# Expert sums in x's place, a fourth buffer for weight parts, and modulation chunks loaded two ahead from ScalarE's queue

## The chip, the cores and the metric

The kernel runs on one core of a Trainium2 chip. A core has TensorE (PE, matmul), VectorE (DVE), ScalarE (ACT), GpSimd (POOL) and SyncE (SP); SP computes nothing here and only issues DMA transfers. Sixteen DMA engines move data between DRAM and the on-chip memory SBUF. The metric is the device time of one execution, in microseconds; less is better.

## The reference

A two-layer network in float32 on T = 256 tokens of width D = 2048, for one sequence. From a conditioning vector c come modulation vectors (shift, scale, gate), as silu(c) times large matrices.

```
def first_block(x, c, ...):
    mod = silu(c) @ w_ada + b_ada
    sh1, sc1, ga1, sh2, sc2, ga2 = split(mod, 6)
    x = x + ga1 * hybrid_mixer(rmsnorm(x) * (1 + sc1) + sh1)
    x = x + ga2 * peer(rmsnorm(x) * (1 + sc2) + sh2)
    return rmsnorm(x, g_final)

def peer(h):   # 8 heads, 128 x 128 product keys, 16 experts kept for each head
    act = gelu(h @ peer_u[chosen].T) * routing_weight
    return act @ peer_v[chosen]
```

Behind it stand an S5 state-space layer with a gated output, then an attention layer with compressed, selected and window branches; each has modulation vectors of its own (mod_w0, mod_w1, kv_mod_w). peer_u and peer_v hold 16,384 experts of 2,048 numbers each, 128 MB apiece.

## The kernel before

The experts are not gathered: the kernel computes all 16,384 of them and multiplies what was not chosen by zero. The work runs in this order (us of the profiled execution): first modulation (0 to 110), the mixer (110 to 590), queries and top-k (590 to 720), gate products of the first expert groups beside the routing tables (720 to 1030), the **V stage** (1030 to 2376), the addition of the expert sums to x (`home`, to 2440), S5 (to 2690), its gate and output and the keys and values (to 3040), attention (to 3616).

In the V stage 16 expert groups alternate: `u_group` (x times peer_u, gelu, routing weight) of a group ahead, then `v_group` (activations times peer_v). `mix` builds a group's activations from gates and a routing table `wd` that comes back from DRAM: GpSimd multiplies (L909), ScalarE rounds (L911), GpSimd takes the rest (L913). The sums of the experts lie in `acc` (tile `vacc`, 16 KB for each partition), to which DVE adds what PE left in PSUM (L937); `home` transposes them and adds them to x.

A float32 weight is used as two rounded parts. `half` (L335) loads 128x1024 numbers, 512 KB, into a `raw` buffer (L339, issued by SP); ScalarE casts it to `wh` (L342); DVE takes the rest, `wl` = raw - wh (L346). PE multiplies by both: in `step_b` by wh on 512 columns (L357) and by wl on 256 (L358), eight such pairs for a half; in `v_group` with three products of 512 columns (L928 to L930), four such triples for a half. I call a 128x1024 piece of a weight a half. `raw` has four buffers, wh and wl three each, `graw` two.

Modulation is computed in the background. `gemv` (L284) is a generator that loads a 128x1024 **chunk** of a modulation matrix into a `graw` buffer (L299, issued by SP) and then adds it, scaled, to the row sums `gacc` on DVE (L312), or multiplies it on PE (L293) in the stage that has no gacc pool. `tick`, called once for every two halves, advances it by a rate: 1.5, later 3 steps in the mixer, and in the V stage as many as spread what is left over 205 ticks. Beside it, `s5_tables` builds 16 tables for S5 in one tile `tb` on DVE and stores each to DRAM (L1193).

The program is written in this order, and a tile scheduler then orders each engine's instructions by priority and estimated time; each engine works through its own list in order, and an instruction that waits holds all that stand behind it.

Of the kernel before, what the change touches and what calls it, by code (L numbers as in the profile page):

```python
# [9 lines left out]
F = mybir.dt.float32  # L10
# [67 lines left out]
COLS = {}  # L78
PAUSE = 2


# [75 lines left out]
class K:  # L157
    def __init__(self, tc, A, dbg=None):
        self.tc, self.nc, self.A = tc, tc.nc, A
        self.dbg = dbg or {}  # L160
        self.full = True
        self.nw, self.pool_share, self.srate = 0, 0, 1
        self.bg, self.side, self.par, self.loads = [], [], [], []
        self.loaded, self.gate, self.gp, self.hold, self.mid = None, None, None, None, False
        self.rate, self.owed, self.sowed, self.towed, self.slow = 1.5, 0.0, 0.0, 0.0, None

# [115 lines left out]


    def gemv(self, w, blocks, which, bias, out, big=False):  # L284
        nc = self.nc
        for b in blocks:
# [9 lines left out]
            for k in range(KD):  # L296
                if not big:
                    raw = self.sb.tile([128, 1024], F, name="graw", tag="graw", bufs=2)
                    nc.sync.dma_start(raw, w[128 * k:128 * k + 128, c0])  # L299
                else:  # L300
                    if k % 4 == 0:
                        rt = self.xs(F).rearrange("p a b t -> p (a b t)").rearrange("p (a c) -> p a c", a=4)
                        self.loads.append(
                            nc.sync.dma_start(rt, w[128 * k:128 * k + 512, c0].rearrange("(a p) c -> p a c", a=4)))
                    raw = rt[:, k % 4]
                ck = self.cact[:, 16 * which + k:16 * which + k + 1]
                if acc is None:
                    columns(ck.to_broadcast([128, 32]), raw, k == 0, k == KD - 1)
                elif k == 0:
                    nc.vector.tensor_scalar(acc, raw, ck, None, op0=OP.mult)  # L310
                else:
                    nc.vector.scalar_tensor_tensor(acc, raw, ck, acc, op0=OP.mult, op1=OP.add)  # L312
                if k < KD - 1:
                    yield True
# [20 lines left out]
    def half(self, src, i):  # L335
        nc = self.nc
        s = self.sb.tile([128, 1024], F, name="raw", tag="raw", bufs=4)
        with self.after(self.gate):
            self.loaded = nc.sync.dma_start(s, src[:, 1024 * i:1024 * i + 1024])  # L339
        h = self.sb.tile([128, 1024], R, name="wh", tag="wh", bufs=3)  # L340
        l = self.sb.tile([128, 1024], R, name="wl", tag="wl", bufs=3)
        nc.scalar.copy(h, s)  # L342
# [405 lines left out]
    def _peer(self, x):  # L748
# [6 lines left out]
        xk = [x[:, k] for k in range(KD)]  # L755
        self.normed(xk, self.rstd(self.accx, D), g, mod[:, 48:64], hs)
        kt = self.t8()
        ktf = kt.rearrange("p a b -> p (a b)")
# [100 lines left out]
        def router():  # L859
# [3 lines left out]
            for q in range(64 + LAG):  # L863
# [11 lines left out]
                if q >= LAG:  # L875
# [10 lines left out]
                    if r % 4 == 3:  # L886
                        nc.sync.dma_start(wd[r // 4], tb.rearrange("p i t -> p (i t)"))
                yield True
# [27 lines left out]
        def v_group(gv, ap):  # L916

            for dq in range(4):
# [13 lines left out]
                for t in range(2):  # L932
                    s = acc[:, t, 512 * dq:512 * dq + 512]
                    if gv == 0:
                        nc.scalar.copy(s, pp[t])
                    else:
                        nc.vector.tensor_add(s, s, pp[t])  # L937
                if gv == 15:
                    self.par.append(home(dq))

        def home(dq):

            yield True
            for k in range(4 * dq, 4 * dq + 4):
                p = self.pm()[:, :T]
                for t in range(2):
                    nc.tensor.transpose(p[:, 128 * t:128 * t + 128], acc[:, t, 128 * k:128 * k + 128], self.ident)
                nc.vector.scalar_tensor_tensor(x[:, k], p, mod[:, 80 + k:81 + k], x[:, k], op0=OP.mult, op1=OP.add)
                self.accx = self.ssq(None if k == 0 else self.accx, x[:, k], k == KD - 1)
# [24 lines left out]
        self.ph = ctx.__enter__()  # L974
        acc = self.ph.tile([128, 2, D], F, name="vacc")
        self.slow = self.s5_tables()
        self.use_pool(self.ph if GP[2] else None)
        if self.full:
            self.pace("m1", VR)
        self.pool_share = VP  # L980
        for gv in range(16):
            nx = None
            if gv + 1 < 16:
                aps[gv + 1] = self.xs()
                nx = mix(gv + 1, gq[gv + 1], aps[gv + 1])
                self.side.insert(0, nx)
# [46 lines left out]
    def s5_setup(self):  # L1033
# [59 lines left out]
        def cmul(o, xr, xi, y):  # L1093

            wr, wi, yr, yi = wide(xr), wide(xi), y[:, :, 0], y[:, :, 1]
            t = self.sb.tile([128, 1024], F, name="graw", tag="graw", bufs=2)
            t = t.rearrange("p (k j c) -> p k j c", k=16, j=4)
# [72 lines left out]
    def s5_tables(self):  # L1170
        nc = self.nc
        for jj in range(16):
# [19 lines left out]
            nc.scalar.activation(tb, tb, AF.Sin, scale=-6.283185)  # L1192
            nc.sync.dma_start(self.s5d[jj][:, :1024], tb.rearrange("p i a b -> p (i a b)"))  # L1193
            yield True
# [193 lines left out]
    def _nsa(self, x):  # L1388
# [27 lines left out]
        def compress(i):  # L1416
            p = self.pm()
            for h in range(4):
                w = sb.tile([128, 1024], F, name="raw", tag="raw", bufs=4)
                nc.sync.dma_start(w, A["cmp_w1"][i][:, 1024 * h:1024 * h + 1024])  # L1420
# [193 lines left out]
```

## Time and profile before

| | |
|---|---|
| median of 3 runs | 3625.65 us (3624.92 to 3626.92) |
| the profiled execution | 3617.7 us, its span 3616.0 us |
| PE busy | 3294.4 us, 91% of the span |
| DVE busy | 2652.5 us, 73% |
| ACT busy | 1700.7 us, 47% |
| POOL busy | 1066.7 us, 29% |
| granted PE clock, mean | 0.961 |
| DMA | 832.47 MB, 230 GB/s over the span |

Busy time counts executing instructions; issuing a DMA is not among them. A matmul's end is modelled, so PE may be slower than it could be while it counts as busy. Idle time of an engine matters only where the engine that sets the pace then waits for it.

### The profile page before, as it was taken

Reading aid. Unit: us, or ns where it says so; the run is one execution under the profiler, and the core shown is the slowest. Engines: PE = TensorE matmul, PEld = TensorE weight load, DVE = VectorE, ACT = ScalarE, POOL = GpSimd, SP = SyncE. Lnnn points to the kernel's source line nnn. Section 1 sums busy time; section 2 is a strip of 40 time slices with the busy share of each in tenths; the row PEclk is TensorE's granted clock in tenths of the full one; section 3 lists DMA queues with packets and bytes.
Section 4 is the critical chain, followed back from the end, with each engine's and each line's share of the span. In section 5 each row is a group of like instructions: output and inputs, shape, how many; then the busy total and the mean of one; then the engine's idle time right before and its main releaser. Section 6 shows DMA issues by size and latency. Waiting matters only on the chain.

```text
span 3616.0 us, 50453 instructions
## 1 busy us (share of the span) xinstructions
PE 3294.4 (91%) x18446; PEld 2726.2 (75%) x18446; DVE 2652.5 (73%) x4072; ACT 1700.7 (47%) x2789; POOL 1066.7 (29%) x892
## 2 busy tenths in 40 slices
PE   4988778999999999999999989988989989999998
PEld 1676666878777777777777777767878878888886
DVE  4778987997657778887777767779886565666665
ACT  1534544455544444554444433354545544555553
POOL 1123345666522121211211233035452320122223
PEclk7999989999999999999999999989999999999999
DMA  9697676567779888888888878744435556444444
GB/s 398 235 301 252 203 234 228 163 223 262 243 250 314 300 281 291 293 285 279 293 286 278 293 268 269 267 158 139 147 127 186 186 167 198 160 155 149 159 143 144
DMA packets 260409, 832.47 MB, mean 230 GB/s; under 512 B 25792, under 2 KB 66880, under 8 KB 257472
## 3 DMA queue, kind: packets, MB, share of 16 engines
q1 hardware_dynamic: 258096, 829.11, 68.0%
q8 instruction: 145, 2.38, 0.3%
q14 instruction: 104, 0.85, 0.1%
q10 hardware_dynamic: 2064, 0.13, 0.0%
HBM read 797.56 MB, written 31.59 MB: 229 GB/s over the span
## 4 chain that ended last, share of the span: by engine, by line
PE 46%; DVE 14%; DMA 13%; issue 6%; POOL 3%; ACT 1%; SPq 0%; DVEq 0%; POOLq 0%; ACTq 0%
PE p L357 22%; PE p L358 11%; DVE wl L346 5%; DMA graw<-mod_w 5%; DMA graw<-kv_mod_w 3%; PE pm L929 2%; PE pm L928 2%; PE pm L930 2%; DVE gacc L312 2%; DMA s5d<-tb 2%; DMA raw<-peer_u 1%; DVE xs L1286 1%; PE pm L882 1%; ACT wh L342 1%; POOL xs L913 1%
## 5 line engine op out<-in xcount | busy, mean ns | idle before, releaser
L357 PE MATMUL p<-xs,wh 128*128 128x512 f32 x5600 | 2038.6, 406 | 43.5 <-DVE xs L476 19.9
L358 PE MATMUL p<-xs,wl 128*128 128x256 f32 x5600 | 1595.6, 285 | 47.6 <-DVE wl L346 40.4
L342 ACT CAST wh<-raw 128x1024 fp32r<-128x1024 f32 x996 | 1038.4, 1048 | 1124.6 <-PE p L357 408.9
L346 DVE TENSOR_TENSOR wl<-raw,wh 128x1024 fp32r<-128x1024 f32 x904 | 1151.4, 1281 | 511.0 <-ACT wh L342 501.4
L357 PEld LDWEIGHTS p<-xs,wh 128*128 128x128 f32 x5600 | 1069.5, 191 | 321.1 <-issue 39.0
L358 PEld LDWEIGHTS p<-xs,wl 128*128 128x128 f32 x5600 | 1078.4, 193 | 74.5 <-DVE wl L346 58.3
L312 DVE SCALAR_TENSOR_TENSOR gacc<-graw,cact,gacc 128x1024 f32<-128x1024 f32 x315 | 448.8, 1425 | 154.5 <-DMA graw<-mod_w 90.2
L929 PE MATMUL pm<-wl,xs 128*128 128x512 f32 x1024 | 411.7, 402 | 25.3 <-DVE wl L346 24.7
L928 PE MATMUL pm<-wh,xs 128*128 128x512 f32 x1024 | 409.4, 400 | 24.2 <-DVE vacc L937 18.8
L930 PE MATMUL pm<-wh,xs 128*128 128x512 f32 x1024 | 405.8, 396 | 0.0
L346 POOL TENSOR_TENSOR wl<-raw,wh 128x1024 fp32r<-128x1024 f32 x92 | 231.8, 2524 | 305.1 <-ACT wh L342 273.1
L909 POOL TENSOR_TENSOR t<-t,t 128x256 f32<-128x256 f32 x128 | 138.3, 1114 | 589.3 <-DMA t<-wd 589.3
L929 PEld LDWEIGHTS pm<-wl,xs 128*128 128x128 f32 x1024 | 196.2, 192 | 85.1 <-DVE wl L346 45.6
L913 POOL TENSOR_TENSOR xs<-t,xs 128x256 fp32r<-128x256 f32 x128 | 150.6, 1207 | 355.0 <-ACT xs L911 354.9
L928 PEld LDWEIGHTS pm<-wh,xs 128*128 128x128 f32 x1024 | 196.0, 191 | 74.9 <-DVE vacc L937 22.1
L930 PEld LDWEIGHTS pm<-wh,xs 128*128 128x128 f32 x1024 | 196.3, 192 | 39.7
L439 POOL TENSOR_TENSOR ssq<-ssq,s 128x256 f32<-128x256 f32 x96 | 105.4, 1107 | 237.7 <-ACT s L435 235.8
L898 ACT ACTIVATE t<-et 128x256 f32<-128x256 f32 x128 | 53.8, 420 | 209.4 <-DVE et L414 209.2
L413 ACT COPY et<-p 128x256 f32<-128x256 f32 x281 | 102.2, 364 | 31.2 <-PE p L358 31.1
L1528 POOL TENSOR_SCALAR t<-t,st 128x128 f32<-128x128 f32 (+1 forms) x64 | 77.6, 1224 | 128.0 <-DVE st L1526 128.0
L872 DVE TENSOR_SCALAR xs<-iof,eT,eT 128x128 f32<-128x128 f32 x192 | 82.2, 487 | 37.9 <-PE pm L882 37.9
L414 DVE TENSOR_TENSOR et<-p,et 128x256 f32<-128x256 f32 x224 | 93.1, 416 | 10.3 <-ACT et L413 10.3
(392 smaller groups left out, 3126.3 us busy)
## 6 DMA issues: line engine op xcount, KB each, us to landing
raw<-peer_u SPq DMA_DIRECT2D x256, 512.0 KB, 5.3
raw<-peer_v SPq DMA_DIRECT2D x256, 512.0 KB, 5.6
graw<-mod_w SPq DMA_DIRECT2D x192, 512.0 KB, 5.6
graw<-w_ada SPq DMA_DIRECT2D x128, 512.0 KB, 4.8
raw<-nsa_z SPq DMA_DIRECT2D x96, 512.0 KB, 3.7
xs<-w_ada SPq DMA_DIRECT2D x16, 2048.0 KB, 13.1
graw<-kv_mod_w SPq DMA_DIRECT2D x64, 512.0 KB, 5.7
raw<-w_out SPq DMA_DIRECT2D x32, 512.0 KB, 5.1
```

Source lines behind the costliest of these rows:

```text
L312: nc.vector.scalar_tensor_tensor(acc, raw, ck, acc, op0=OP.mult, op1=OP.add)
L342: nc.scalar.copy(h, s)
L346: (nc.gpsimd if on_pool else nc.vector).tensor_sub(l, s, h.bitcast(F))
L357: self.nc.tensor.matmul(p, h[:, sl], x, start=k == 0, stop=False, skip_group_check=True)
L358: self.nc.tensor.matmul(p[:, 1], l[:, sl], x[:, 0], start=False, stop=k == KD - 1, skip_group_check=True)
L413: nc.scalar.copy(t, p[:, 0])
L439: nc.gpsimd.tensor_add(acc[0], acc[0], sq)
L909: nc.gpsimd.tensor_mul(gc, gc, wv[:, c])
L913: nc.gpsimd.tensor_sub(ap[:, c - 2, 1], gs[:, c - 2], ap[:, c - 2, 0].bitcast(F))
L928: nc.tensor.matmul(pp[t], ah, h[:, sl], start=c == 0, stop=False, skip_group_check=True)
L929: nc.tensor.matmul(pp[t], ah, l[:, sl], start=False, stop=False, skip_group_check=True)
L930: nc.tensor.matmul(pp[t], ap[:, c, 1, 128 * t:128 * t + 128], h[:, sl], start=False, stop=c == 7, skip_group_check=True)
```

## The change

First, the expert sums no longer have a tile of their own. At the start of `_peer`, once the normalized x has been formed, ScalarE's queue stores x (2 MB) to a DRAM tile `xd`, and `acc` becomes a view of x's tile. Before the second-last `v_group` two 1 MB loads on SP's queue bring x back into two tiles `xin`, and `home` reads x from there. Second, the room goes into buffers: `raw` 5, `wh` and `wl` 4, `graw` 3. Third, `fetch_chunk` takes the chunk loads out of `gemv`'s loop: they are issued by ScalarE instead of SP, and two chunks (DEEP) are kept ahead of the one in use. The stores of the routing tables (wd) and of the S5 tables are moved to ScalarE's queue too.

```diff
+DEEP = 2
+    def fetch_chunk(self):
+        if self.chunks:
+            src = self.chunks.pop(0)
+            raw = self.sb.tile([128, 1024], F, name="graw", tag="graw", bufs=3)
+            self.nc.scalar.dma_start(raw, src)
+            self.ahead.append(raw)
...
     def gemv(self, w, blocks, which, bias, out, big=False):
+        if not big:
+            self.chunks += [w[128 * k:128 * k + 128, 1024 * b:1024 * b + 1024] for b in blocks for k in range(KD)]
...
                 if not big:
-                    raw = self.sb.tile([128, 1024], F, name="graw", tag="graw", bufs=2)
-                    nc.sync.dma_start(raw, w[128 * k:128 * k + 128, c0])
+                    while not self.ahead:
+                        self.fetch_chunk()
+                    raw = self.ahead.pop(0)
...
                     nc.vector.scalar_tensor_tensor(acc, raw, ck, acc, op0=OP.mult, op1=OP.add)
+                if not big:
+                    while len(self.ahead) < DEEP and self.chunks:
+                        self.fetch_chunk()
...
     def half(self, src, i):
-        s = self.sb.tile([128, 1024], F, name="raw", tag="raw", bufs=4)
+        s = self.sb.tile([128, 1024], F, name="raw", tag="raw", bufs=5)
-        h = self.sb.tile([128, 1024], R, name="wh", tag="wh", bufs=3)
-        l = self.sb.tile([128, 1024], R, name="wl", tag="wl", bufs=3)
+        h = self.sb.tile([128, 1024], R, name="wh", tag="wh", bufs=4)
+        l = self.sb.tile([128, 1024], R, name="wl", tag="wl", bufs=4)
...
+        xd = self.dr.tile([128, KD, T], F, name="xd")
+        nc.scalar.dma_start(xd, x)
+        acc = x.rearrange("p k (t c) -> p k t c", t=2)
...
-                        nc.sync.dma_start(wd[r // 4], tb.rearrange("p i t -> p (i t)"))
+                        nc.scalar.dma_start(wd[r // 4], tb.rearrange("p i t -> p (i t)"))
...
-        acc = self.ph.tile([128, 2, D], F, name="vacc")
...
+            if gv == 14:
+                for h in range(2):
+                    xin.append(self.t8())
+                    nc.sync.dma_start(xin[h], xd[:, 8 * h:8 * h + 8])
...
-            nc.sync.dma_start(self.s5d[jj][:, :1024], tb.rearrange("p i a b -> p (i a b)"))
+            nc.scalar.dma_start(self.s5d[jj][:, :1024], tb.rearrange("p i a b -> p (i a b)"))
```

The change moves instructions on every engine, since the scheduler orders all anew. First SP, in the V stage, where the loads for the last part of one expert group meet those of the next (about half 480 of 996). Before, the chunk loads (graw) and an S5 table's store (s5d) stand between the weights' loads (raw):

```order
L299 DMA graw<-mod_w 128x1024
L339 DMA raw<-peer_v 128x1024
L1193 DMA s5d<-tb 128x1024
L339 DMA raw<-peer_v 128x1024 x4
L299 DMA graw<-mod_w 128x1024
L339 DMA raw<-peer_u 128x1024
L299 DMA graw<-mod_w 128x1024
L339 DMA raw<-peer_u 128x1024
L299 DMA graw<-mod_w 128x1024
L339 DMA raw<-peer_u 128x1024
```

The same place on SP after the change, where t<-wd is the load of a routing table:

```order
L359 DMA raw<-peer_v 128x1024 x16
L359 DMA raw<-peer_u 128x1024 x10
L927 DMA t_16687<-wd 128x16x128
L359 DMA raw<-peer_u 128x1024 x6
L359 DMA raw<-peer_v 128x1024 x16
```

SP's queue holds only weights and routing tables there; the chunk loads and the store have left it. Second, ScalarE at the same half 480, before, where xs<-t is a rounding of `mix`, s<-pg, et<-p and t<-et small copies and the gelu:

```order
L324 COPY s_15762<-pg 128x256
L342 CAST wh<-raw 128x1024 x5
L911 CAST xs<-t_12537 128x256
L342 CAST wh<-raw 128x1024
L911 CAST xs<-t_12537 128x256 x5
L342 CAST wh<-raw 128x1024
L911 CAST xs<-t_12537 128x256 x2
L342 CAST wh<-raw 128x1024
```

After the change:

```order
L344 COPY s_15767<-pg 128x256
L291 DMA graw<-mod_w 128x1024
L362 CAST wh<-raw 128x1024
L291 DMA graw<-mod_w 128x1024 x2
L362 CAST wh<-raw 128x1024
L291 DMA graw<-mod_w 128x1024
L362 CAST wh<-raw 128x1024
L291 DMA graw<-mod_w 128x1024
L362 CAST wh<-raw 128x1024
L291 DMA graw<-mod_w 128x1024
L362 CAST wh<-raw 128x1024
```

A chunk load now stands ahead of each of these casts. Each waits until DVE has used the chunk that lay in its buffer three chunks earlier. Third, SP at the end of the gate products, where only peer_v is left, before (the second part begins 32 halves further on):

```order
L339 DMA raw<-peer_u 128x1024
L339 DMA raw<-peer_v 128x1024
L903 DMA t_18336<-wd 128x16x128
L339 DMA raw<-peer_v 128x1024 x2
L903 DMA t_18697<-wd 128x16x128
...
L339 DMA raw<-peer_v 128x1024 x2
L903 DMA t_19067<-wd 128x16x128
L339 DMA raw<-peer_v 128x1024 x3
L903 DMA t_19431<-wd 128x16x128
```

After the change, with t_18341, t_18702, t_19072 and t_19440 the same four routing tables:

```order
L359 DMA raw<-peer_u 128x1024 x10
L927 DMA t_18341<-wd 128x16x128
L359 DMA raw<-peer_u 128x1024 x2
L927 DMA t_18702<-wd 128x16x128
L359 DMA raw<-peer_u 128x1024 x3
L927 DMA t_19072<-wd 128x16x128
L359 DMA raw<-peer_u 128x1024
L359 DMA raw<-peer_v 128x1024 x2
L1012 DMA t_19433<-xd 128x2048
L359 DMA raw<-peer_v 128x1024 x3
L1012 DMA t_19435<-xd 128x2048
L359 DMA raw<-peer_v 128x1024 x8
```

Three of the four tables are loaded earlier, ahead of the last gate products, the two loads of x stand where two tables stood, and the fourth table (t_19440) follows behind these rows.

## Rows read from the trace of the kernel before

**Rows 1.** Windows: length, busy PE, PEld, DVE, ACT, POOL, PE clock, DMA share, GB/s.

```profile
0.00:110.00 110.00, 57.49 (x554) 28.88 (x556) 51.22 (x174) 30.46 (x86) 11.04 (x21) 0.78 0.93 366
110.00:590.00 480.00, 394.15 (x2112) 323.98 (x2104) 392.79 (x558) 214.00 (x382) 163.08 (x97) 0.93 0.75 249
...
1030.00:2080.00 1050.00, 990.70 (x4966) 809.03 (x4967) 816.29 (x936) 487.91 (x661) 193.50 (x164) 0.99 0.85 289
2080.00:2240.00 160.00, 142.17 (x579) 111.10 (x579) 114.14 (x102) 60.13 (x80) 64.39 (x61) 0.93 0.79 263
2240.00:2376.00 136.00, 134.02 (x605) 108.42 (x604) 95.50 (x100) 56.29 (x66) 12.26 (x14) 1.00 0.75 255
```

**Rows 2.** PE timeline inside a gate and an expert group: start, duration.

```profile
1180.76 0.40 PE L357 MATMUL p<-xs,wh 128*128 128x512 f32 x1
...
1181.11 0.40 PE L357 MATMUL p<-xs,wh 128*128 128x512 f32 x1
...
2240.33 0.39 PE L928 MATMUL pm<-wh,xs 128*128 128x512 f32 x1
...
2241.01 0.39 PE L928 MATMUL pm<-wh,xs 128*128 128x512 f32 x1
```

**Rows 3.** PE by line, 1030 to 2080: busy, mean ns, idle before, releaser.

```profile
L357 PE MATMUL p<-xs,wh 128*128 128x512 f32 x1431 | 510.0, 399 | 0.0
L358 PE MATMUL p<-xs,wl 128*128 128x256 f32 x1431 | 408.2, 285 | 25.8 <-DVE wl L346 25.2
...
L928 PE MATMUL pm<-wh,xs 128*128 128x512 f32 x640 | 254.0, 398 | 11.4 <-DVE vacc L937 11.2 <-ACT wh L342 0.2
```

**Rows 4.** The same by line in 2080 to 2240, then in 2240 to 2376.

```profile
L928 PE MATMUL pm<-wh,xs 128*128 128x512 f32 x186 | 77.3, 415 | 11.8 <-DVE vacc L937 6.6 <-ACT wh L342 5.2
...
L928 PE MATMUL pm<-wh,xs 128*128 128x512 f32 x190 | 74.9, 394 | 1.0 <-DVE vacc L937 0.9
```

**Rows 5.** The chain that ended last, by line, 1030 to 2080 us.

```profile
by line: DMA graw<-mod_w 13.6%; PE p L357 11.5%; DVE wl L346 11.4%; DMA graw<-kv_mod_w 9.4%; issue 8.4%; PE p L358 6.3%; DMA s5d<-tb 5.7%; DVE gacc L312 5.0%; DMA raw<-peer_u 4.9%; PE pm L929 3.9%; PE pm L928 3.9%; PE pm L930 3.8%; DMA raw<
```

**Rows 6.** Pieces of that chain in 1180 to 1300: start, us, what.

```profile
1201.39 6.54 DMA graw<-mod_w
1208.02 1.30 DVE gacc L312
1209.34 5.23 DMA graw<-mod_w
```

**Rows 7.** Waits of the SP queue, 1030 to 2376: us, times, longest.

```profile
SPq L299 <- DVE gacc L312: 128.0, 97, 3.7
SPq L299 <- DMA graw<-mod_w: 67.4, 48, 4.3
```

**Rows 8.** Waits of DVE and then ACT, 1030 to 2376.

```profile
DVE wl L346 <- ACT wh L342: 149.9, 116, 6.7
...
DVE tb L1178 <- DMA s5d<-tb: 24.0, 10, 5.1
...
ACT xs L911 <- POOL t L909: 19.8, 16, 4.5
```

**Rows 9.** DVE and ACT by line, 1030 to 2376.

```profile
L342 ACT CAST wh<-raw 128x1024 fp32r<-128x1024 f32 x433 | 452.0, 1049 | 517.5 <-PE pm L930 332.3 <-PE p L357 66.6 <-DMA raw<-peer_v 63.2
...
L312 DVE SCALAR_TENSOR_TENSOR gacc<-graw,cact,gacc 128x1024 f32<-128x1024 f32 x225 | 301.9, 1342 | 131.7 <-DMA graw<-mod_w 90.2 <-DMA graw<-kv_mod_w 40.2
```

**Rows 10.** DMA issues, 1030 to 2376: count, KB each, median us to landing.

```profile
graw<-mod_w SPq DMA_DIRECT2D x183, 512.0 KB, 5.6
...
t<-wd SPq DMA_DIRECT2D x14, 1024.0 KB, 9.2
```

**Rows 11.** The one DMA that ACT issues: durations ns min/median/max.

```profile
L1147 ACTq DMA_DIRECT2D s5d<-direct x1: 389/389/389, 120.4 to 120.4; - x1
```

**Rows 12.** Waits of DVE in 110 to 590, then PE in 590 to 1030.

```profile
DVE gacc L312 <- DMA graw<-w_ada: 22.6, 17, 2.8
...
PE pg L293 <- DMA graw<-w_ada: 6.3, 4, 2.3
```

More of the change, by code (lines that the diff above doesn't have):

```diff
@@ L164, in __init__ @@
         self.loaded, self.gate, self.gp, self.hold, self.mid = None, None, None, None, False
+        self.ahead, self.chunks = [], []
         self.rate, self.owed, self.sowed, self.towed, self.slow = 1.5, 0.0, 0.0, 0.0, None
@@ L281, in consts, with _gemv @@
         nc.vector.tensor_scalar(self.cact, self.cact, 0.5, None, op0=OP.mult)
-    def gemv(self, w, blocks, which, bias, out, big=False):
+    def fetch_chunk(self):
[4 more added lines that the diff above has]
+            self.ahead.append(raw)
+    def gemv(self, w, blocks, which, bias, out, big=False):
+        nc = self.nc
+        if not big:
+            self.chunks += [w[128 * k:128 * k + 128, 1024 * b:1024 * b + 1024] for b in blocks for k in range(KD)]
+        return self._gemv(w, blocks, which, bias, out, big)
+    def _gemv(self, w, blocks, which, bias, out, big):
         nc = self.nc
@@ L932, in v_group @@
                 for t in range(2):
-                    s = acc[:, t, 512 * dq:512 * dq + 512]
+                    s = acc[:, 4 * dq:4 * dq + 4, t]
+                    p = pp[t].rearrange("p (k c) -> p k c", k=4)
                     if gv == 0:
-                        nc.scalar.copy(s, pp[t])
+                        nc.scalar.copy(s, p)
                     else:
-                        nc.vector.tensor_add(s, s, pp[t])
+                        nc.vector.tensor_add(s, s, p)
                 if gv == 15:
@@ L946, in home @@
                 for t in range(2):
-                    nc.tensor.transpose(p[:, 128 * t:128 * t + 128], acc[:, t, 128 * k:128 * k + 128], self.ident)
-                nc.vector.scalar_tensor_tensor(x[:, k], p, mod[:, 80 + k:81 + k], x[:, k], op0=OP.mult, op1=OP.add)
+                    nc.tensor.transpose(p[:, 128 * t:128 * t + 128], acc[:, k, t], self.ident)
+                nc.vector.scalar_tensor_tensor(x[:, k], p, mod[:, 80 + k:81 + k], xin[k // 8][:, k % 8],
+                                               op0=OP.mult, op1=OP.add)
                 self.accx = self.ssq(None if k == 0 else self.accx, x[:, k], k == KD - 1)
@@ L980, in _peer @@
         self.pool_share = VP
+        xin = []
         for gv in range(16):
             nx = None
+            if gv == 14:
+                for h in range(2):
+                    xin.append(self.t8())
+                    nc.sync.dma_start(xin[h], xd[:, 8 * h:8 * h + 8])
             if gv + 1 < 16:
@@ L1095, in cmul @@
             wr, wi, yr, yi = wide(xr), wide(xi), y[:, :, 0], y[:, :, 1]
-            t = self.sb.tile([128, 1024], F, name="graw", tag="graw", bufs=2)
+            t = self.sb.tile([128, 1024], F, name="graw", tag="graw", bufs=3)
             t = t.rearrange("p (k j c) -> p k j c", k=16, j=4)
@@ L1418, in compress @@
             for h in range(4):
-                w = sb.tile([128, 1024], F, name="raw", tag="raw", bufs=4)
+                w = sb.tile([128, 1024], F, name="raw", tag="raw", bufs=5)
                 nc.sync.dma_start(w, A["cmp_w1"][i][:, 1024 * h:1024 * h + 1024])
```

## The prediction

> **What bounds the kernel now.** I read the windows by stage first, then PE by line in the long stage, then the chain and the waits there. In the V stage, 1030 to 2376 us, PE is busy 991 of 1050 us, 142 of 160 and 134 of 136 [rows 1]. Busy is not the same as fast, so I set PE's own floor beside it. Undisturbed, the pairs of a gate product start 0.35 us apart and the triples of an expert group 0.68 us (1180.76 to 1181.11, 2240.33 to 2241.01) [rows 2]; a half is 8 pairs or 4 triples, 2.8 or 2.7 us. In 1030 to 2080 stand 1431 pairs and 640 triples [rows 3]: 1431 x 0.35 + 640 x 0.68 = 936 us of 1050. Some 20 us of the rest I leave to the small products of the modulation, my estimate; 94 us are lost. In 2080 to 2240 the 186 triples need 126 us of 160, and in 2240 to 2376 the 190 need 129 of 136 [rows 4]; with the same allowance in proportion, 30 and 3 are lost. So **127 us** can be won in this stage, and no more.
>
> What PE waits for at its own queue is wl (25.8 us for the gates' products) and the expert sums (11.4) [rows 3]. What is late behind these is in the chain: chunk loads graw hold 13.6% and 9.4% of it, more than any other line [rows 5]. Its pieces show a loop: a chunk takes 6.54 us to land, DVE adds it in 1.30, and 0.02 us after that the next lands in 5.23 more [rows 6]. It is a loop because there are two graw buffers, and it reaches PE because SP waits in it: SP's chunk issues waited 128 us for DVE to free a buffer and 67 us for a transfer [rows 7], with the weights' loads queued behind them. DVE in turn waited 149.9 us for casts [rows 8] and 131.7 us for chunks [rows 9], and wl stands in the same queue.
>
> **The change part by part.**
>
> *Third chunk buffer, loads two ahead.* Two buffers gave two chunks for each landing (5.6 us [rows 10]), addition (1.34 [rows 9]) and issue, 0.4: 7.4 us, or 3.7 us for a chunk. Three give 2.5 us. PE takes 2.75 us for a half. Where chunks alternate with halves, as in the order of SP before, 3.7 was too slow and 2.5 is not. On average there are 225 chunks to 433 casts [rows 9], so the loop binds in runs of chunks, not throughout. That is why I do not count all of 127 as won.
>
> *From SP to ScalarE.* SP no longer waits in front of a weight load, so loads run as far ahead as five raw buffers allow. The price is on ScalarE: each chunk load costs it the 0.39 us that its only DMA took [rows 11], 247 of them and some 16 of tables near 105 us. With 488 us busy of 1050 [rows 1] it has room. What is queued behind a waiting load there is the cast, and DVE's wl behind the cast. The load waits for the addition of the chunk three back; as ScalarE's new order shows, it stands one or two casts behind that addition, 2.7 to 5.5 us, which covers the addition itself. I take nothing for it and keep the rival below.
>
> The Trainium skill speaks against this part: "DMA: Bandwidth & Descriptors", section "Issuing engines are not separate DMA queues", says that transfers run on the same 16 engines whoever issues them, and that another issuer saves only issue time. By that rule the move alone is worth nothing and only the buffers count; were they half of the term for the V stage below, 38 us, the time would be 3575 us. SP's 128 us and 67 us of waiting ahead of an issue [rows 7] are neither transfer nor issue time, so the trace does not agree that nothing else is saved.
>
> *Four wh and wl, five raw.* With three wh buffers, a cast starts when PE ends with the half three before, and two halves of cover, 5.5 us, stand against cast 1.05 [rows 9], subtraction 1.3 and whatever DVE does first. A fourth makes it 8.2 us. The longest wait of wl for a cast was 6.7 us [rows 8], which lies between the two. This and the loop attack the same loss, so they get one term.
>
> *x in DRAM.* The store is 2 MB and each load back 1 MB, at 9.2 us for 1 MB [rows 10]: 18 us and twice 9 us of transfer beside products that last hundreds of us. The two t8 tiles and three routing tables taken earlier change the border at 2080 to 2240: ScalarE waited 19.8 us for GpSimd's products there [rows 8], and multiplications now run ahead of the roundings. I count that within the 30 us of this window. If a landing of x held ScalarE's loads uncovered, it would cost up to 9 us; I take 0.
>
> *Table stores.* DVE waited 24.0 us, 10 times, for tb to be stored [rows 8]. SP issued a store some three loads early; ScalarE's new order puts it a cast later. 16 waits of 5 us instead of 2.4 would be 40 us of DVE time, covered by four wl buffers where they don't meet other delays.
>
> *Sum for the V stage*: six tenths of 127, **-76 us**. The six tenths is my choice. The floor of what can go is the chunk waits that reach PE straight (25.8 of wl), the ceiling 127. I am nearer the ceiling because all four parts work on one loss, but not at it, since 2240 to 2376 ran almost at the floor with the old buffers and DVE at 70%, while 1030 to 2080 had it at 78% [rows 1]: part of the loss is DVE's load, and that stays.
>
> *Mixer, 110 to 590*: DVE waited 22.6 us for chunks [rows 12] at 82% busy [rows 1]. I take 13 of it as won and 5 lost where six chunk loads stand in a row on ScalarE early in the stage (from the order; two halves): **-8 us**, between +10 and -22. *Gates beside the tables, to 1030*: PE itself waited 6.3 us for chunks [rows 12]: **-5**, between 0 and -12. *After 2376* there are no chunks: 0, give or take 5.
>
> -76 - 8 - 5 = -89 us: 3617.7 - 89 = 3529 for the profiled execution. The median of the timed runs lies 8 us above that execution, so 3625.65 - 89 = **3537 us**.
>
> **Rivals.**
>
> *A: DVE becomes the bound.* DVE does the same work in a shorter stage: 816 us of, say, 990 is 82%. With the table waits at 5 us it is 86%, its queue has little slack, and PE goes on waiting for wl. What speaks for it is the contrast of 70% and 78% above. A third of 127 goes, 42 us: 3584 us.
>
> *B: nearly everything goes.* Four buffers smooth all bursts: -127 - 22 - 12 = -161: 3465 us. For it: PE's waits are short and many, just what a buffer hides; against: DVE at 82%.
>
> *C, slower: ScalarE's queue is held.* A chunk load that waits now holds casts. Three chunks take landing + 2.1 us (0.39 issue, 1.34 addition, some 0.3 between), three halves 8.25, so this decides above a landing of 6.1 us where chunks and casts alternate. Weights loaded deeper ahead share the engines with the chunks: 289 GB/s would become some 307 in 990 us, against 366 at a share of 0.93 in the first 110 us [rows 1]. If the landing rose from 5.6 to 8 us, each run of three chunks would lose 1.85 us of ScalarE and PE, in half of 75 runs 70 us, with the old loss kept because casts come late: 3660 to 3696 us.
>
> *D: nothing moves.* If what stretches the stage is landing time alone, and DVE's order puts each chunk where it is waited for anyway, PE waits as before: 3619 to 3633 us. For it speaks that a landing takes 5.6 us of the 7.4 of a loop [rows 10]; against it, that two chunks in flight are now three. The rule of the Trainium skill named above points this way for the move alone.
>
> **How the numbers follow.** The forecast, -50 to -120, gets 0.50; A 0.20; B 0.13; C 0.10; D 0.07. Its own range is 3505 to 3576. Within 0.2%, 7 us, a measurement can't tell the two kernels apart: only D lies there. Faster: 0.50 + 0.20 + 0.13 = 0.83; same 0.07; slower 0.10. The range is 3460 to 3605: all of the forecast, nearly all of A, most of B, near 0.8.
>
> **What would show it.** Right: the V stage ends near 2300 us; chunk loads fall from 23% to under 10% of its chain; DVE's 131.7 us for chunks fall below 50; wl waits on PE below 15; ScalarE some 105 us of issuing and no more than 20 us behind a load. A would show DVE above 85% and waits for tb near 5 us each. C would show a landing above 6.1 us and casts idle behind a chunk load. A mixer more than 10 us longer would make that term wrong, and PE held at 2080 to 2240 by xs or by x's landing the border.

## The result, and the profile after

The changed kernel takes 3576.09 us (median of 4 runs, 3570.07 to 3585.38), the kernel before 3625.28 in the same measurement: 0.9868 of it, interval [0.9844, 0.9892], so 49 us less. The profiled execution has a span of 3571.7 us against 3616.0, a difference of 44.3 us, and that is the one I take apart.

It isn't one gain. Two lines of PE mark where the stages stand: the first score product of the expert layer (L797, after the change L821), which ends the mixer and the queries, and the first and the last triple of the expert groups (L928, now L952). Here they are before, with the durations of one in ns and, behind them, first and last start in us:

```profile
L797 PE MATMUL pm<-t,xs x64: 270/275/377, 618.5 to 700.9; 128*128 128x128 f32 x64
...
L928 PE MATMUL pm<-wh,xs x1024: 386/389/796, 1097.4 to 2382.2; 128*128 128x512 f32 x171
```

And after:

```profile
L821 PE MATMUL pm<-t,xs x64: 270/275/377, 647.7 to 731.3; 128*128 128x128 f32 x64
...
L952 PE MATMUL pm<-wh,xs x1024: 387/389/792, 1126.9 to 2341.3; 128*128 128x512 f32 x171
```

The mixer ends 29.2 us later (647.7 for 618.5). From there to the first triple nothing changes (478.9 and 479.2 us). The V stage, from the first triple to the last, falls from 1284.8 to 1214.4 us: **70.4 us won**. What follows is 3.4 us shorter. 29.2 + 0.3 - 70.4 - 3.4 = -44.3. The same window from first to last triple, before and then after (columns as in [rows 1]):

```profile
1097.40:2382.20 1284.80, 1209.77 (x5801) 983.87 (x5800) 986.56 (x1080) 576.39 (x769) 273.76 (x242) 0.98 0.84 282
1126.90:2341.30 1214.40, 1180.47 (x5801) 978.21 (x5800) 987.01 (x1089) 571.01 (x768) 281.98 (x238) 0.99 0.85 296
```

PE runs the same 5801 instructions. It is idle 41.1 us less (75.0 and 33.9), and its busy time is 29.3 us shorter, so waiting that the profile doesn't show as idle went too; the granted clock, 0.98 and then 0.99, can be a part of that, and how large a part stays open.

The windows answer to [rows 1]; the stages have shifted inside them by up to 45 us:

```profile
110.00:590.00 480.00, 380.34 (x2004) 312.38 (x2004) 372.49 (x548) 202.19 (x374) 142.49 (x87) 0.90 0.71 239
1030.00:2080.00 1050.00, 1007.14 (x5151) 836.19 (x5150) 854.68 (x971) 499.97 (x691) 248.28 (x206) 0.99 0.86 302
2080.00:2240.00 160.00, 156.16 (x691) 127.17 (x690) 127.71 (x119) 67.02 (x84) 43.62 (x34) 0.99 0.84 293
2240.00:2376.00 136.00, 119.36 (x526) 96.64 (x526) 94.06 (x128) 58.49 (x85) 22.21 (x32) 0.91 0.53 180
```

In 1030 to 2080 PE and DVE are both busier, and the DMA engines move 302 GB/s instead of 289. In the chain of 1030 to 2080 us the chunk loads no longer lead, with 12.7% instead of 23% [rows 5]:

```profile
by line: PE p L377 15.6%; PE pm L952 9.9%; PE pm L953 9.8%; PE pm L954 9.8%; PE p L378 8.3%; DMA graw<-mod_w 7.4%; DVE wl L366 7.2%; issue 6.8%; DVE gacc L329 5.4%; DMA graw<-kv_mod_w 5.3%; POOL t L933 2.3%; DMA s5d<-tb 2.0%; DVE x L962 1.1
```

PE's waits for wl and for the sums, by line in 1030 to 2376 us, answer to [rows 3, 4] (the sums are x's tile now):

```profile
L378 PE MATMUL p<-xs,wl 128*128 128x256 f32 x1511 | 430.1, 285 | 16.1 <-DVE wl L366 16.1
...
L952 PE MATMUL pm<-wh,xs 128*128 128x512 f32 x1024 | 404.4, 395 | 19.1 <-DVE x L962 17.5 <-DVE m L351 1.4
L953 PE MATMUL pm<-wl,xs 128*128 128x512 f32 x1024 | 401.5, 392 | 2.0 <-DVE wl L366 2.0
```

Before, the expert groups' line had as much to wait for wl in this window as the gates' line with its 25.8 [rows 3]:

```profile
L929 PE MATMUL pm<-wl,xs 128*128 128x512 f32 x1015 | 408.2, 402 | 25.3 <-DVE wl L346 24.7
```

So the waits for wl fell from some 50 us to 18.1; the sums still cost 17.5. SP hardly waits for chunks any more, but for a raw buffer, which DVE frees when it has formed wl:

```profile
SPq L359 <- DVE wl L366: 906.6, 353, 29.0
```

That long wait is a good one: it says that a load is issued the moment a buffer is free. DVE's waits in the same window [rows 8, 9]:

```profile
DVE wl L366 <- ACT wh L362: 150.3, 125, 4.1
DVE gacc L329 <- DMA graw<-mod_w: 46.8, 37, 3.9
DVE gacc L329 <- DMA graw<-kv_mod_w: 19.2, 14, 4.4
...
DVE tb L1208 <- DMA s5d<-tb: 14.0, 8, 2.9
```

The wait for chunks fell from 131.7 to 67.2 us by line, of which these two are 66.0; that for a stored table from 24.0 to 14.0. ScalarE's queue has a new wait, a cast behind a chunk load that waits for its buffer:

```profile
ACT wh L362 <- DVE gacc L329: 59.3, 22, 5.8
```

The DMA issues [rows 10], and the time that ScalarE's queue took to issue one (min, median and max in ns) [rows 11]:

```profile
graw<-mod_w ACTq DMA_DIRECT2D x183, 512.0 KB, 5.9
...
graw<-kv_mod_w ACTq DMA_DIRECT2D x64, 512.0 KB, 6.4
t<-wd SPq DMA_DIRECT2D x14, 1024.0 KB, 10.3
...
t<-xd SPq DMA_DIRECT2D x2, 1024.0 KB, 5.8
```

```profile
L291 ACTq DMA_DIRECT2D graw<-mod_w x192: 334/334/617, 941.9 to 2259.3; - x192
L291 ACTq DMA_DIRECT2D graw<-w_ada x128: 334/334/1502, 86.4 to 932.5; - x128
```

### The profile page after: what moved, and what is told of

Its sections match the earlier page's. It is cut to its first block, busy times and chain, and to the rows that moved or that the text cites. A ratio compares the mean times of both kernels' runs of the same rounds, so it can differ in the third digit from the quotient of the medians.

```text
span 3571.7 us, 50594 instructions
## 1 busy us (share of the span) xinstructions
PE 3260.8 (91%) x18446; PEld 2722.1 (76%) x18446; DVE 2658.8 (74%) x4072; ACT 1689.1 (47%) x2787; POOL 1077.1 (30%) x892
## 4 chain that ended last, share of the span: by engine, by line
PE 61%; DVE 18%; DMA 11%; issue 5%; POOL 3%; ACT 2%; DVEq 0%; ACTq 0%; SPq 0%; POOLq 0%
PE p L377 24%; PE p L378 12%; PE pm L952 5%; PE pm L953 5%; PE pm L954 5%; DVE wl L366 5%; DMA graw<-w_ada 3%; DVE gacc L329 3%; DMA graw<-mod_w 3%; DMA graw<-kv_mod_w 2%; PE pm L906 1%; DVE xs L1316 1%; PE pg L309 1%; DMA raw<-w_k 1%; ACT wh L362 1%
## 5 line engine op out<-in xcount | busy, mean ns | idle before, releaser
L329 DVE SCALAR_TENSOR_TENSOR gacc<-graw,cact,gacc 128x1024 f32<-128x1024 f32 x315 | 441.0, 1400 | 113.2 <-DMA graw<-mod_w 46.8
L952 PE MATMUL pm<-wh,xs 128*128 128x512 f32 x1024 | 404.4, 395 | 19.1 <-DVE x L962 17.5
L953 PE MATMUL pm<-wl,xs 128*128 128x512 f32 x1024 | 401.5, 392 | 2.0 <-DVE wl L366 2.0
L954 PE MATMUL pm<-wh,xs 128*128 128x512 f32 x1024 | 400.9, 391 | 0.0
L937 POOL TENSOR_TENSOR xs<-t,xs 128x256 fp32r<-128x256 f32 x128 | 157.9, 1262 | 728.0 <-ACT xs L935 727.6
L952 PEld LDWEIGHTS pm<-wh,xs 128*128 128x128 f32 x1024 | 193.3, 189 | 67.0 <-DVE x L962 20.4
L933 POOL TENSOR_TENSOR t<-t,t 128x256 f32<-128x256 f32 x128 | 150.8, 1212 | 164.1 <-DMA t<-wd 164.1
```

The source lines that it names most:

```text
L933: nc.gpsimd.tensor_mul(gc, gc, wv[:, c])
L937: nc.gpsimd.tensor_sub(ap[:, c - 2, 1], gs[:, c - 2], ap[:, c - 2, 0].bitcast(F))
L952: nc.tensor.matmul(pp[t], ah, h[:, sl], start=c == 0, stop=False, skip_group_check=True)
L953: nc.tensor.matmul(pp[t], ah, l[:, sl], start=False, stop=False, skip_group_check=True)
L954: nc.tensor.matmul(pp[t], ap[:, c, 1, 128 * t:128 * t + 128], h[:, sl], start=False, stop=c == 7, skip_group_check=True)
```

## The experiments

For each I give the time (the ratios are to runs of the kernel before on the same chip, whose medians were 3625.97, 3621.01 and 3620.93 for e1 to e4, e5 to e8 and e9 to e12), and from the profiled execution two lengths taken at the lines above: the first score product (618.5 us before) and the V stage, first triple to last (1284.8).

| kernel | median us | ratio to before, interval | first score product | V stage |
|---|---|---|---|---|
| before | 3625.28 | | 618.5 | 1284.8 |
| the change | 3576.09 | 0.9868 [0.9844, 0.9892] | 647.7 | 1214.4 |
| e1 chunks from SP | 3577.96 | 0.9883 [0.9852, 0.9914] | 638.7 | 1227.0 |
| e2 SP, then ScalarE in the V stage | 3562.52 | 0.9829 [0.9803, 0.9855] | 635.4 | 1216.7 |
| e3 old weight buffers | 3618.81 | 0.9986 [0.9967, 1.0004] | 645.8 | 1250.1 |
| e4 weight buffers alone | 3627.17 | 1.0008 [0.9995, 1.0022] | 620.4 | 1292.0 |
| e5 as e2, ahead in the V stage only | 3540.30 | 0.9781 [0.9765, 0.9797] | 617.5 | 1210.3 |
| e6 as e5, wh and wl 3 | 3580.65 | 0.9890 [0.9874, 0.9907] | 621.0 | 1243.3 |
| e7 as e5, raw 4 | 3569.97 | 0.9861 [0.9845, 0.9877] | 630.1 | 1224.5 |
| e8 as e5, every fourth wl on GpSimd | 3666.25 | 1.0126 [1.0109, 1.0143] | 617.4 | 1331.8 |
| e9 as e5, one ahead | 3548.88 | 0.9791 [0.9766, 0.9816] | 620.6 | 1223.0 |
| e10 as e5, none ahead | 3541.09 | 0.9772 [0.9747, 0.9798] | 621.2 | 1217.3 |
| e11 as e5, all from SP | 3561.26 | 0.9834 [0.9804, 0.9864] | 621.4 | 1234.0 |
| e12 as e5, two chunk buffers in the mixer | 3561.10 | 0.9833 [0.9806, 0.9859] | 624.7 | 1210.4 |

The two lengths come from one execution each. Where the program up to there is the same (e5 and e8 to e11) the first score products lie 4.0 us apart (617.4 to 621.4); smaller differences say nothing.

My first theory was that the V stage won by the chunk loop and the mixer lost by ScalarE's queue. What speaks for the second half is DVE's wait for chunks in 110 to 590 us, which doubled from 22.6 [rows 12]:

```profile
DVE gacc L329 <- DMA graw<-w_ada: 45.3, 25, 4.2
```

**e1, chunk loads from SP everywhere**

```diff
-            self.nc.scalar.dma_start(raw, src)
+            self.nc.sync.dma_start(raw, src)
```

> The changed kernel with its chunk loads issued by SP instead of ScalarE; two ahead, three chunk buffers, all other buffers as changed. Theory Q (the mixer got 29 us longer because its chunk loads stand in ScalarE's queue behind small steps that wait for DVE and PE): the mixer's end (start of the 784th gate-or-projection pair on PE) returns to within 8 us of the kernel before (594.6 us; 627.4 in the changed kernel). In the V stage SP waits for chunk buffers again, so of the 66 us won there some 20 are lost: near 3570 us. Rival R (the loss comes from loading two ahead and from the new order, whoever issues): the mixer stays 25 to 35 us longer and the time is 3575 to 3600 us.

Neither theory fits. The first score product comes at 638.7 us, 9 earlier than in the change but 20 later than before. The V stage loses 12.6 of its 70 us. Counted in PE's timeline from 0, as all pairs and triples below, the 784th pair starts at 617.6, between 594.6 and 627.4. And 57.8 of the 70.4 us are won with every chunk still issued by SP, which waited 111.9 us in those issues.

**e2, from SP up to the V stage, from ScalarE in it**

```diff
-            self.nc.scalar.dma_start(raw, src)
+            (self.nc.scalar if self.late else self.nc.sync).dma_start(raw, src)
```

`late` is set just ahead of the V stage's loop.

> The changed kernel with chunk loads from SP up to the V stage, from ScalarE in it. Theory Q: the mixer loses nothing (within 8 us of before), the V stage keeps its 66 us: 3545 to 3558 us. Rival R: the mixer stays 25 to 35 us longer, 3570 to 3580 us.

The V stage keeps its gain, as theory Q said, but the mixer gets back only 12.3 us of 29.2. DVE's wait for chunks there falls from the change's 45.3 us to below the 22.6 of before, so that part was the queue's:

```profile
DVE gacc L329 <- DMA graw<-w_ada: 10.1, 12, 2.5
```

Some 17 us of the loss have nothing to do with who issues. Against e1, which differs only in who issues in the V stage, ScalarE's queue is worth 10.3 us there.

**e3, the old weight buffers, and e4, the new ones alone**

```diff
-        s = self.sb.tile([128, 1024], F, name="raw", tag="raw", bufs=5)
+        s = self.sb.tile([128, 1024], F, name="raw", tag="raw", bufs=4)
-        h = self.sb.tile([128, 1024], R, name="wh", tag="wh", bufs=4)
-        l = self.sb.tile([128, 1024], R, name="wl", tag="wl", bufs=4)
+        h = self.sb.tile([128, 1024], R, name="wh", tag="wh", bufs=3)
+        l = self.sb.tile([128, 1024], R, name="wl", tag="wl", bufs=3)
```

> The changed kernel with the old four raw and three wh and wl buffers: chunk loads from ScalarE two ahead alone. Theory L (the chunk loop is the larger part of the V stage's gain): the V stage still wins 35 to 50 us of 66, the mixer loses its 29: 3590 to 3605 us. Rival B (the fourth wh and wl and the fifth raw buffer give most): the V stage wins under 25 us, 3610 us or more.

e4 keeps these buffers as changed and puts the chunks back:

```diff
-                    while not self.ahead:
-                        self.fetch_chunk()
-                    raw = self.ahead.pop(0)
+                    raw = self.sb.tile([128, 1024], F, name="graw", tag="graw", bufs=2)
+                    nc.sync.dma_start(raw, w[128 * k:128 * k + 128, c0])
...
-                        nc.scalar.dma_start(wd[r // 4], tb.rearrange("p i t -> p (i t)"))
+                        nc.sync.dma_start(wd[r // 4], tb.rearrange("p i t -> p (i t)"))
```

> Five raw, four wh and wl, x in DRAM, but chunks as before (SP, two buffers, none ahead) and table stores on SP. Theory L: the V stage wins 15 to 30 us, the mixer stays within 8 us of before: 3595 to 3610 us. Rival B: the V stage wins 45 us or more, 3580 us or less.

The new chunk loading alone wins 34.7 us in the V stage, just at the edge of what theory L allowed. Its time, 3618.81, lies in rival B's range all the same: with 29 us lost and 35 to 50 won, theory L should have said 3605 to 3620. The buffers alone win nothing there (7.2 us longer), which no theory had. Together they win 70.4, so the parts don't add up. In e4 SP stood at chunks for longer than before, against 128 and 67 us [rows 7]:

```profile
SPq L315 <- DVE gacc L328: 175.3, 115, 4.5
...
SPq L315 <- DMA graw<-mod_w: 82.1, 56, 4.9
```

With the shorter waits for chunks of kv_mod_w and for the first addition of a block that is 294.8 us. PE's wait for the sums, 18.8 us before and 17.5 in the change, also grew; why was not tried:

```profile
PE pm L948 <- DVE x L958: 39.3, 7, 8.1
```

**e5, as e2, with chunks ahead in the V stage only**

```diff
-                    while len(self.ahead) < DEEP and self.chunks:
+                    while self.late and len(self.ahead) < DEEP and self.chunks:
```

> The changed kernel with chunks loaded as before up to the V stage (SP, none ahead; three buffers), and from ScalarE two ahead in the V stage. Theory P (loading ahead lets the scheduler put chunk additions on DVE earlier, between the steps on which the mixer's PE waits): the mixer's end comes within 8 us of the kernel before, as with the buffers alone (599.4 us); the wait of PE for the normalized input of the output projection falls from 18 to 13 us or less; the V stage keeps its 70 us: 3545 to 3560 us. Rival S (the 20 us that stay in the mixer with SP come from the buffers or another order): the mixer stays 15 us or more longer, 3560 to 3575 us.

3540.3 us, the fastest kernel of the study: 81 us below the kernel before in the same measurement (3621.01), and 36 below the change, which was measured at another time (32 by the ratios). Both markers:

```profile
L821 PE MATMUL pm<-t,xs x64: 270/275/377, 617.5 to 701.2; 128*128 128x128 f32 x64
...
L952 PE MATMUL pm<-wh,xs x1024: 387/389/795, 1101.9 to 2312.2; 128*128 128x512 f32 x171
```

The mixer is back (617.5 for 618.5) and the V stage is 74.5 us shorter. But the way was not the expected one. I had seen where the change lost in the mixer: between the sum of squares and the normalized input xs (L496, before L476) DVE runs a chain of short steps, on which the output projection waits. In the stretch of that chain before (476.5 to 486.3 us), by line, stood four chunk additions, the first of them begun ahead of the chain, at 475.41 (the wait in its row is from there too):

```profile
L312 DVE SCALAR_TENSOR_TENSOR gacc<-graw,cact,gacc 128x1024 f32<-128x1024 f32 x4 | 5.1, 1280 | 2.5 <-DMA graw<-w_ada 2.5
L465 DVE SCALAR_TENSOR_TENSOR rstd<-s,rstd 128x256 f32<-128x256 f32 x3 | 1.3, 426 | 0.1
```

And after (489.7 to 506.1), seven, all inside the chain, which lasts 16.4 us instead of 9.8:

```profile
L329 DVE SCALAR_TENSOR_TENSOR gacc<-graw,cact,gacc 128x1024 f32<-128x1024 f32 x7 | 9.0, 1281 | 1.9 <-DMA graw<-w_ada 1.8
...
L485 DVE SCALAR_TENSOR_TENSOR rstd<-s,rstd 128x256 f32<-128x256 f32 x3 | 1.3, 420 | 0.0
```

PE's wait there, in 440 to 520 us of the change, has a longest piece of 18.0 us, for 12.6 before. Here is before, then the change:

```profile
PE p L357 <- DVE xs L476: 19.9, 2, 12.6
...
PE p L377 <- DVE xs L496: 27.0, 2, 18.0
```

In e5 it stayed as long:

```profile
PE p L377 <- DVE xs L496: 21.9, 2, 18.3
```

Seven additions stand in its chain too (466.4 to 483.5). So at this place it is not the loading ahead. The mixer came back because earlier stretches ran faster: the 400th pair starts 16 us earlier than before, and the later ones are still longer than before. Against e2, the 17.9 us lie in the first 272 pairs (5.9), between the 400th and the 560th (5.3) and from there to the 784th (6.9), with 1.7 ahead of them and 1.9 lost elsewhere.

**e6, three wh and wl, and e7, four raw**

```diff
-        h = self.sb.tile([128, 1024], R, name="wh", tag="wh", bufs=4)
-        l = self.sb.tile([128, 1024], R, name="wl", tag="wl", bufs=4)
+        h = self.sb.tile([128, 1024], R, name="wh", tag="wh", bufs=3)
+        l = self.sb.tile([128, 1024], R, name="wl", tag="wl", bufs=3)
```

> As the kernel with chunks ahead in the V stage only, but wh and wl with three buffers, raw with five. Theory W (the fourth wh and wl are what the chunks ahead need to give their gain, since a cast waits for PE to free wh): of the 70 us of the V stage some 35 are left, near 3590 us. Rival L5 (the fifth load buffer is what matters): the V stage loses under 10 us, below 3565 us.

> As the kernel with chunks ahead in the V stage only, but raw with four buffers, wh and wl with four. Theory W: the V stage loses under 10 us, below 3565 us. Rival L5: 25 us or more are lost, near 3590 us.

The V stage is 33.0 us longer with three wh and wl, as theory W said, and 14.2 longer with four raw, which lies between the theories; e7's mixer also ends 12.6 us later, which the theories left out. What the fourth wh and wl buy shows on PE: its waits for wl in 1030 to 2330 us in e6,

```profile
PE p L378 <- DVE wl L366: 33.8, 20, 4.4
PE pm L953 <- DVE wl L366: 13.3, 14, 3.1
```

and in e5:

```profile
PE p L378 <- DVE wl L366: 13.7, 15, 4.9
...
PE pm L953 <- DVE wl L366: 5.0, 5, 2.1
```

**e8, every fourth subtraction on GpSimd**

```diff
-VP = 0
+VP = 1
```

> As the kernel with chunks ahead in the V stage only, but GpSimd takes every fourth subtraction wl in the V stage, some 108 of 433. Theory D (what is left of the V stage's loss, some 57 us, is DVE's load): DVE is spared 108 x 1.29 = 139 us and the V stage gets 15 to 40 us shorter. Rival N (the rest is not DVE's): no more than 8 us either way, or longer, since GpSimd takes twice as long for one.

121.5 us longer in the V stage than e5. It doesn't settle theory D. For one thing, DVE was hardly relieved, since the rest of its work got slower. In the V stage of e5 and then of e8 (first to last triple), by line:

```profile
L366 DVE TENSOR_TENSOR wl<-raw,wh 128x1024 fp32r<-128x1024 f32 x418 | 543.7, 1307 | 141.4 <-ACT wh L362 139.7 <-PE p L377 0.9
L329 DVE SCALAR_TENSOR_TENSOR gacc<-graw,cact,gacc 128x1024 f32<-128x1024 f32 x212 | 290.2, 1369 | 64.2 <-DMA graw<-mod_w 46.5 <-DMA graw<-kv_mod_w 16.8
...
L366 DVE TENSOR_TENSOR wl<-raw,wh 128x1024 fp32r<-128x1024 f32 x314 | 444.5, 1418 | 221.8 <-ACT wh L362 221.3
L329 DVE SCALAR_TENSOR_TENSOR gacc<-graw,cact,gacc 128x1024 f32<-128x1024 f32 x213 | 332.5, 1561 | 76.5 <-DMA graw<-mod_w 49.4 <-DMA graw<-kv_mod_w 25.3 <-DVE gacc L329 0.3
```

A subtraction went from 1.31 to 1.42 us and an addition from 1.37 to 1.56, so DVE was busy 968.0 us instead of 983.2, 15 us less and not 139. For another, a new wait came: GpSimd takes 2.74 us for one, as long as PE for a half,

```profile
L366 POOL TENSOR_TENSOR wl<-raw,wh 128x1024 fp32r<-128x1024 f32 x108 | 296.0, 2741 | 697.6 <-ACT wh L362 697.6
```

and PE waits for it:

```profile
PE p L378 <- POOL wl L366: 67.3, 13, 12.9
...
PE pm L953 <- POOL wl L366: 10.6, 1, 10.6
```

**e9 and e10, one chunk ahead and none, in the V stage**

```diff
-DEEP = 2
+DEEP = 1
```

e10 has DEEP = 0 in the same place.

> As the kernel with chunks ahead in the V stage only, but one chunk ahead instead of two; three buffers, ScalarE's queue. Theory H (the chunk must be issued well before its addition, so depth matters): the V stage, 74.6 us shorter with two ahead (first to last triple of the expert groups), is 40 to 65 us shorter; 3550 to 3575 us. Rival T (a third buffer is enough): within 8 us of two ahead, 3533 to 3548 us.

> The same with no chunk ahead: ScalarE issues a chunk's load in the loop, three buffers. Theory H: the V stage is at most 35 us shorter than before; 3575 us or more. Rival T: 60 us or more shorter, below 3555 us.

Theory H falls with e10: with none ahead the V stage is 67.5 us shorter than before, the time 3541.09. e9 by itself lies between the theories: its 61.8 us are in H's range, its 3548.88 just above T's. One ahead is no better than none, so the differences among the three, up to 12.7 us, don't follow depth; I put them down to the new order, which no run shows by itself. A likely reason is in ScalarE's timeline in e10: while gate products run (1617 to 1660 us), 13 chunk loads stand among 14 casts there too, so with three buffers the scheduler places the loads early by itself.

**e11, the V stage's chunks from SP**

```diff
-            (self.nc.scalar if self.late else self.nc.sync).dma_start(raw, src)
+            self.nc.sync.dma_start(raw, src)
```

> The kernel with chunks two ahead in the V stage only, but its chunk loads there issued by SP. Theory Z (ScalarE's queue is worth some 12 us in the V stage, since SP waits in a chunk issue with weights behind it; the two runs with SP and then ScalarE differ by that much there): 3548 to 3558 us, SP waiting over 60 us in chunk issues in 1030 to 2330 us. Rival E (the queue is worth nothing, the difference was order): within 5 us of 3540 us.

21 us slower than e5, the V stage 23.7 us longer, twice what e1 against e2 gave (10.3). It is still 58.0 us shorter than in e4, where SP issued the chunks too, with two buffers and none ahead, and the tables' stores as well. SP waits in chunk issues again, 109.6 us:

```profile
SPq L291 <- DVE gacc L329: 81.8, 59, 4.0
SPq L291 <- DVE gacc L327: 17.8, 12, 2.3
...
SPq L291 <- DMA graw<-mod_w: 10.0, 5, 6.5
```

**e12, two chunk buffers up to the V stage**

```diff
+            third = self.late and self.nf % 3 == 2
+            self.nf += self.late
+            tag = "graw3" if third else "graw"
-            raw = self.sb.tile([128, 1024], F, name="graw", tag="graw", bufs=3)
+            raw = self.sb.tile([128, 1024], F, name="graw", tag=tag, bufs=1 if third else 2)
```

> The kernel with chunks two ahead in the V stage only, with two chunk buffers up to the V stage and the third joining in it. Theory M (the third buffer alone moves some four chunk additions ahead of the mixer's normalized output: 80 instead of 75 or 76 additions by the 560th pair): by that pair 74 to 77 additions are done, the stretch from the 400th to the 560th pair takes 115 to 120 us instead of 126.7, and the time is 3528 to 3538 us. Rival: the stretch stays above 124 us, 3537 to 3550 us.

At the place theory M holds: by the 560th pair 75 additions are done, the stretch from the 400th pair takes 118.0 us, and PE's wait there is as short as before:

```profile
PE p L380 <- DVE xs L499: 14.8, 2, 11.1
```

For the time it fails. The first 272 pairs take 171.3 us instead of 159.2, and those from the 560th to the 784th 113.7 instead of 107.4: the third buffer wins before and behind the output projection more than it loses at it. Another 5.8 us are lost behind the V stage, where a temporary tile of S5 shares the chunks' buffers and has two again instead of three. That part lasts 1225.3 to 1230.7 us in the eight kernels that have the same program there, and 1232.2 here, so most of the 5.8 us can be spread.

## Why the prediction was right, and where it was off

The sum gave 3537 us, the measurement 3576.09: inside the stated range, at the very edge of the forecast's own (3505 to 3576). The gain came where the sum had put it, in the V stage, nearly in full; of the 44 us by which the profiled execution exceeded the sum (3573.3 for 3529), 37 are the mixer's. That the total still fell inside is owed to the width of the range and not to the mixer's term.

**The V stage: right.** The floor of PE (127 us to be won; with its own allowance the last window has 4 and not 3) and six tenths of it gave -76; measured -70.4. The six tenths was a choice, so that it came this close is partly luck. One row was read too narrowly: the 25.8 us of waiting for wl are the gates' line alone. That the chunk loop binds is shown by e4: with the old loop the new weight buffers gain nothing. That a part of it reached PE through SP's queue is shown by e1 against e2 (10.3 us) and e11 against e5 (23.7). The larger part doesn't hang on the queue: with SP issuing, three chunk buffers and two ahead, together with the tables' stores moved, take the V stage from 1292.0 (e4) to 1234.0 (e11) and 1227.0 (e1), and SP's waits in chunk issues from 294.8 to 109.6 and 111.9 us. That the fourth wh and wl count is shown by e6, 33.0 us, and the fifth raw by e7, 14.2. One term for all was the right choice, since they don't add: chunk loading alone (e3) has -34.7, weight buffers alone (e4) +7.2, both together -70.4.

**Loading ahead: the reason was wrong.** I gave the loop's 2.5 us for a chunk to the buffer and the loading ahead together. e10 shows that depth is worth nothing that can be told from the order (7 us), on ScalarE's queue. If that holds on SP's too, most of the 58 us between e4 and e11 is the third buffer's; it was not taken away by itself in the V stage, so its own share stays open.

**From SP to ScalarE: right that the rule is not all.** The rule of the Trainium skill on issuing engines ("DMA: Bandwidth & Descriptors", section "Issuing engines are not separate DMA queues") allowed the move only issue time. Measured were 23.7 us in the V stage (e11) and 10.3 (e1 against e2), and SP's waits of 109.6 and 111.9 us in chunk issues are what goes away. The landing itself did not get shorter (5.9 us for 5.6 [rows 10]), and in that the trace agrees with the rule. My argument had a flaw: the 67 us of SP's waits are waits for a transfer, so only the 128 us are neither transfer nor issue time. I took nothing for casts behind a waiting load and expected under 20 us of it; it was 59.3 us, 22 times. PE's waits for wl fell all the same.

**The mixer: this step failed.** "I take 13 of it as won and 5 lost [...]: -8 us, between +10 and -22." The first score product, which also has the start and the queries before it, came 29.2 us later, and PE's 784th pair, at the mixer's end, 32.8 us later. The loss lies late: from the 400th to the 560th pair 23.9 us (138.5 for 114.6) and from there to the 784th 14.1 (116.2 for 102.1, where the granted clock was 0.91 for 0.97), while the stretches before the 400th were 9.5 shorter. I had counted the wait of DVE for chunks as something that prefetching removes; it doubled to 45.3 us. In the mixer ScalarE's own small steps wait for GpSimd and DVE (38.3 and 21.9 us for the two largest), and a chunk load that stands behind one must wait as well. e2 takes the mixer's loads off ScalarE's queue and gets 12.3 us back. Not loading ahead gets another 17.9 (e2 to e5), spread over the mixer; by what mechanism I did not find: the place that I suspected waits as long in e5. The additions that stand in the normalization chain come with the third buffer, as e12 shows, and cost 8.7 us at their place (126.7 to 118.0, from the 400th to the 560th pair), but the third buffer wins more than that in the stretches around it.

**Gates and tables, and after 2376: small and wrong or right.** -5 against +0.3; 0 against -3.4, which is within the spread of this last part among kernels that have the same program there (1225.3 to 1230.7 us).

**The rivals.** The time fell beside A's number (3584), but not by A's mechanism: DVE was busy 81% of the V stage (987.0 of 1214.4 us) and not above 85%, tb was waited for 14.0 us, not 80 as 16 waits of 5 us would be, and the V stage won more than half as much again as A's 42 us. A gain of the size that I forecast and a loss that I didn't have add up to it. C's wait came (59.3 us on ScalarE), and the chunks of kv_mod_w landed in 6.4 us, above its 6.1, but it did not decide; that its threshold left out the cover of four wh and wl is my reading, not shown. B and D did not come; the buffers alone, e4, are the kernel that moves nothing.

**The border at 2080 to 2240.** From the 640th to the 768th triple of L928, 111.3 us before and 97.6 after; e4, with old chunk loading but the same two loads of x, took 109.6. So x in DRAM costs nothing visible here, and part of the V stage's gain lies at this place.

Of the signs named: the V stage ends at 2341, not near 2300, since the mixer ends late; chunk loads hold 12.7% of the chain, not under 10; DVE's wait for chunks 67, not under 50; wl on PE 18, not under 15. Each went the right way and stopped short. ScalarE's 247 chunk issues took 0.334 us each, 82 us for the 96 that the prediction had in its 105; it waited 59.3 us behind a load and not under 20.

What stays open: by what mechanism loading ahead cost 17.9 us in the mixer, how far the rest of the V stage's excess, 127 - 70 = 57 us, is DVE's, since e8 hardly relieved it and brought its own wait, and the share of the third chunk buffer alone.

## What to carry to other kernels

A queue that waits holds everything behind it, so a background load should stand in a queue whose next instruction can wait; which one that is differs by stage: here ScalarE's in the V stage (10 to 24 us won) and SP's in the mixer (9 to 12 us). Buffers along one path have to be tried together: more weight buffers alone gave +7.2 us, while the loop of two chunk buffers still held SP for 295 us; the new chunk loading alone gave -34.7; both together -70.4, of which 57.8 came even with SP issuing. And a background task that gets another buffer is also placed earlier, between the steps that the foreground waits for.

## What the runs showed of the hardware beyond that

An issue on ScalarE's queue took 0.334 us (median of 192 and of 128), not the 0.39 of the one DMA [rows 11]. Two transfers of 1 MB each to SBUF landed in 5.8 us for x and 10.3 us for a routing table (medians in the same window); x comes in pieces of 8 KB and the table in pieces of 128 numbers, 512 B; that this is the cause was not tried.

DVE was slower while GpSimd worked: in e5, from 1100 to 2400 us, a subtraction wl on DVE took 1.22 us (median of 319) when GpSimd was idle all through it and 1.75 us (median of 77) when GpSimd was busy nearly all through it.
